# Moving the start address of one class of TensorE operands from 192 to 64 bytes (modulo 512) behind the next stationary tile

## The chip, the cores and the metric

The program runs on one core of a Trainium2 chip. The metric is device time in microseconds of one execution; the median of three runs of the kernel before is 938.64 us.

## What is computed

Four residual layers on a sequence of 256 tokens of width 1024, batch 1, all in float32. Layer 0 mixes with gated linear attention, layer 1 with differential attention; each is followed by a SwiGLU feed-forward block (width 2816) and a gated per-layer-embedding block. Then come a short gated convolution and a causal attention with linear biases and an output gate. Cut to what matters here:

```python
def swiglu(h, w_in, w_out):
    g, u = split_cols(h @ w_in, [D_FF, D_FF])
    return (jax.nn.silu(g) * u) @ w_out

q, k, v, r, zf, zb = split_cols(h @ w_in, ...)      # gated linear attention
q, k, v = split_cols(h @ w_in, ...)                 # differential attention
h = h + mixer(rms_norm(h, g), ...)
```

Almost all arithmetic is in the products of a 256 x 1024 (or 256 x 2816) activation with a weight matrix. The kernel keeps float32 accuracy by splitting both sides in a high part (rounded to the matmul format fp32r) and a low part (the rest), and adding three products: high x high, high x low, low x high.

## The kernel before

Weights come from HBM in pieces ("units") of at most 128 x 1024 values on SP's queue into the tile `raw` (`load`, L151). ScalarE rounds a piece into the high part `whi` (`high`, L165, instruction at L169), VectorE subtracts it from the piece for the low part `wlo` (`low`, L173, instruction at L178). Both run some units ahead of TensorE. A table of due times (`DL`) sets where the elementwise steps of a mixer stand between the units. None of this order depends on an address.

`gemm` (L227) turns a weight matrix into units. A unit of four 256-column pieces gives 24 matmuls: four pieces, two halves `s`, and three products in `mm3` (L222 to L225). There are two forms. In the usual form the weights are stationary (128 x 128 tiles of `whi` and `wlo`) and the activations move (`xh`, `xl`, 256 columns). In the `natural` form, used where the result must have tokens on partitions, it is the other way round: a 128 x 128 tile of `xh` or `xl` is stationary and 256 columns of `whi` or `wlo` move. The natural form is used for four chunks of `gla_i` (the values of the first mixer), all twelve of `diff_i` and twelve of `moba_i`: 28 chunks of two units, each with 24 matmuls, so 448 times the triple

- L223: stationary `xh`, moving `whi`
- L224: stationary `xh`, moving `wlo`
- L225: stationary `xl`, moving `whi`

TensorE loads the stationary tile of a matmul (LDWEIGHTS, PEld in the profile) while the matmul before it still streams its moving operand. In the program's names, `g<-whi,xh` has the moving operand first.

`shifted` (L159) places the weight tiles. Each gets 1152 values (4608 bytes, nine times 512) and begins at an offset `o` in its slot, so that all buffers of a pool have the same start modulo 512. With `DIST = 192` and `SLOT = 512` the moving weights begin 192 bytes into the slot; stationary weights begin at 512 - 192 = 320 bytes, so that the activations that move over them, at 0, are again 192 bytes behind them modulo 512. The activation tiles `xh` and `xl`, and all slices of 128 columns in them, begin at multiples of 512 bytes; a piece of 256 columns is 1024 bytes. So every matmul of both forms moves an operand that begins 192 bytes (modulo 512) behind the stationary tile that is loaded meanwhile. The score products of the attention stages use the same `mm3` with `kh`, `kl` moving over `qh`, `ql`; those tiles all begin at multiples of 512 bytes, a distance of 0.

Of the kernel before, what the change touches and what calls it, by code (L numbers as in the profile page):

```python
# [86 lines left out]
DIST = 192  # L87
SLOT = 512
# [7 lines left out]
def body(ctx: ExitStack, tc: tile.TileContext, a, out: bass.AP):  # L96
# [62 lines left out]
    def shifted(pool, name, u):  # L159
        key, j = seq[u][:2]  # L160
        moving = key == "diff_i" or key == "gla_i" and 4 <= j < 8 or key == "moba_i" and j < 12
        o = (DIST if moving else SLOT - DIST) // 4
        return pool.tile([P, CW // 2 + SLOT // 4], F32R, tag=name, name=name)[:, o:o + CW // 2]

    def high():  # L165
        u = state["hi"]
        key, j, k0, kn, c = seq[u]
        hi = shifted(whip, "whi", u)
        nc.scalar.copy(hi[:, :kn * c], raws[u][:, :kn * c])  # L169
        his[u] = hi  # L170
        state["hi"] += 1

    def low():  # L173
        u = state["lo"]
        key, j, k0, kn, c = seq[u]
        hi = his.pop(u)
        lo = shifted(wlop, "wlo", u)
        nc.vector.tensor_sub(lo[:, :kn * c], raws.pop(u)[:, :kn * c], hi[:, :kn * c].bitcast(F32))  # L178
        ready[u] = [(hi[:, k * c:(k + 1) * c], lo[:, k * c:(k + 1) * c]) for k in range(kn)]
        state["lo"] += 1  # L180
# [1247 lines left out]
```

## Time and profile before

| | us |
|---|---|
| median of 3 runs (lowest, highest) | 938.64 (937.60, 939.99) |
| the profiled execution's own time | 937.24 |
| its span | 935.1 |
| TensorE busy in the span | 913.7 |
| VectorE busy | 663.4 |
| ScalarE busy | 556.2 |
| GpSimd busy | 107.3 |
| mean granted TensorE clock | 0.992 |

The profile is one execution of the program. The duration of a matmul in it includes its latency and overlaps that of the next; how long one really takes of TensorE's time is the distance between two starts, which the timeline shows. That distance is called a step below. The chain of waits names, from the end backwards, what each instruction waited for last.

### The profile page before, as it was taken

How to read it: one execution, taken by the hardware profiler on the slowest of the kernel's cores; microseconds unless marked ns; L12 is line 12 of the kernel's file. 1: busy time of each engine (PE TensorE's matmuls, PEld its weight loads, DVE VectorE, ACT ScalarE, POOL GpSimd, SP SyncE). 2: the span in 40 equal slices, each digit the busy share in tenths (PEclk: the TensorE clock that was granted, in tenths of full speed). 3: DMA queues.
4: the chain of work that ended last, by engine and by line, in shares of the span. 5: the costliest groups of instructions: out<-in, count | busy, mean ns of one | idle time of the engine just before them, and what ended most of it. 6: DMA issues, size and time to landing. Idle time of an engine off the chain costs nothing.

```text
span 935.1 us, 19090 instructions
## 1 busy us (share of the span) xinstructions
PE 913.7 (98%) x7812; PEld 900.6 (96%) x7812; DVE 663.4 (71%) x1000; ACT 556.2 (59%) x951; POOL 107.3 (11%) x74
## 2 busy tenths in 40 slices
PE   9889999999999989899999999999999999999998
PEld 8889999999999989899999999999999999999998
DVE  5884768666656698998587666566897668876663
ACT  5945757455444565677585545444774445777862
POOL 0050310000001352211010000012210003000010
PEclk9989999999999998999999999999999999999999
DMA  8543366655555734343466555565556546644332
GB/s 243 200 138 107 109 205 230 211 189 195 181 189 190 241 127 149 122 141 108 146 217 215 199 193 193 177 200 195 168 206 201 192 132 205 186 134 136 113 114 90
DMA packets 48151, 161.10 MB, mean 172 GB/s; under 512 B 5472, under 2 KB 6368, under 8 KB 48064
## 3 DMA queue, kind: packets, MB, share of 16 engines
q1 hardware_dynamic: 47376, 158.81, 51.7%
q8 instruction: 61, 1.00, 0.4%
q10 hardware_dynamic: 688, 1.07, 0.4%
q14 instruction: 26, 0.21, 0.1%
HBM read 158.81 MB, written 1.05 MB: 171 GB/s over the span
## 4 chain that ended last, share of the span: by engine, by line
PE 81%; DVE 10%; ACT 4%; POOL 2%; issue 2%; DMA 2%; SPq 0%; ACTq 0%; POOLq 0%; DVEq 0%
PE g L223 25%; PE g L225 24%; PE g L224 24%; DVE wlo L178 3%; ACT whi L169 1%; PE m L223 1%; PE m L818 1%; DVE xl L305 1%; PE m L996 1%; DMA h<-in_xT 1%; PE m L1196 1%; PE m L653 1%; ACT xh L301 1%; PE m L224 1%; DVE q L600 1%
## 5 line engine op out<-in xcount | busy, mean ns | idle before, releaser
L223 PE MATMUL g<-xh,whi 128*128 128x256 f32 (+1 forms) x1672 | 465.7, 279 | 1.3 <-ACT whi L169 0.7
L225 PE MATMUL g<-xh,wlo 128*128 128x256 f32 (+1 forms) x1672 | 462.5, 277 | 0.2
L224 PE MATMUL g<-xl,whi 128*128 128x256 f32 (+1 forms) x1672 | 462.4, 277 | 0.1
L178 DVE TENSOR_TENSOR wlo<-raw,whi 128x1024 fp32r<-128x1024 f32 (+2 forms) x315 | 377.3, 1203 | 80.3 <-PE g L225 43.8
L169 ACT CAST whi<-raw 128x1024 fp32r<-128x1024 f32 (+2 forms) x315 | 312.0, 996 | 117.6 <-PE g L224 93.4
L223 PEld LDWEIGHTS g<-xh,whi 128*128 128x128 f32 (+1 forms) x1672 | 314.1, 188 | 2.4 <-ACT whi L169 1.0
L225 PEld LDWEIGHTS g<-xh,wlo 128*128 128x128 f32 (+1 forms) x1672 | 313.8, 188 | 0.6 <-DVE wlo L178 0.6
L224 PEld LDWEIGHTS g<-xl,whi 128*128 128x128 f32 (+1 forms) x1672 | 313.7, 188 | 0.6 <-DVE xl L305 0.3
L223 PE MATMUL g<-whi,xh 128*128 128x256 f32 x448 | 130.8, 292 | 3.5 <-ACT xh L301 3.5
L225 PE MATMUL g<-whi,xl 128*128 128x256 f32 x448 | 127.1, 284 | 0.2 <-DVE xl L305 0.2
L224 PE MATMUL g<-wlo,xh 128*128 128x256 f32 x448 | 126.9, 283 | 0.0
L223 PEld LDWEIGHTS g<-whi,xh 128*128 128x128 f32 x448 | 86.8, 194 | 5.2 <-ACT xh L301 4.0
L225 PEld LDWEIGHTS g<-whi,xl 128*128 128x128 f32 x448 | 86.6, 193 | 0.6 <-DVE xl L305 0.6
L224 PEld LDWEIGHTS g<-wlo,xh 128*128 128x128 f32 x448 | 86.5, 193 | 0.0
L494 ACT ACTIVATE t<-t 128x256 f32<-128x256 f32 x44 | 18.5, 420 | 85.7 <-DVE t L482 85.6
L223 PE MATMUL g<-ah,whi 128*128 128x256 f32 x224 | 61.8, 276 | 0.0
L224 PE MATMUL g<-al,whi 128*128 128x256 f32 x224 | 61.8, 276 | 0.0
L225 PE MATMUL g<-ah,wlo 128*128 128x256 f32 x224 | 61.8, 276 | 0.0
L482 DVE TENSOR_TENSOR t<-g,rb 128x256 f32<-128x256 f32 x44 | 18.6, 424 | 52.1 <-PE g L225 52.0
L305 DVE SCALAR_TENSOR_TENSOR xl<-h,small,xh 128x256 fp32r<-128x256 f32 x64 | 36.6, 610 | 17.1 <-ACT xh L301 17.1
L301 ACT ACTIVATE xh<-h,small 128x256 fp32r<-128x256 f32 x64 | 29.3, 503 | 32.1 <-DVE h L466 7.9
L379 POOL TENSOR_TENSOR h<-h,pj 128x512 f32<-128x512 f32 x8 | 12.9, 1621 | 276.6 <-DVE h L395 270.8
(224 smaller groups left out, 1010.0 us busy)
## 6 DMA issues: line engine op xcount, KB each, us to landing
raw<-in_ffn_i SPq DMA_DIRECT2D x88, 512.0 KB, 4.6
raw<-in_ffn_o SPq DMA_DIRECT2D x40, 512.0 KB, 4.0
raw<-in_conv_i SPq DMA_DIRECT2D x32, 512.0 KB, 4.6
raw<-in_moba_i SPq DMA_DIRECT2D x32, 512.0 KB, 3.8
raw<-in_diff_i SPq DMA_DIRECT2D x24, 512.0 KB, 3.8
raw<-in_gla_i SPq DMA_DIRECT2D x23, 512.0 KB, 5.1
raw<-in_ple_g SPq DMA_DIRECT2D x16, 512.0 KB, 4.7
raw<-in_gla_o SPq DMA_DIRECT2D x5, 512.0 KB, 4.0
```

The costliest lines, as they stand in the source:

```text
L169: nc.scalar.copy(hi[:, :kn * c], raws[u][:, :kn * c])
L178: nc.vector.tensor_sub(lo[:, :kn * c], raws.pop(u)[:, :kn * c], hi[:, :kn * c].bitcast(F32))
L223: nc.tensor.matmul(ps, lh, rh, start=first, stop=False, **kw)
L224: nc.tensor.matmul(ps, lh, rl, start=False, stop=False, **kw)
L225: nc.tensor.matmul(ps, ll, rh, start=False, stop=last, **kw)
L301: nc.scalar.activation(xh[:, j], h[:, j], AF.Copy, scale=gain[j])
L305: nc.vector.scalar_tensor_tensor(xl[:, j], h[:, j], gain[j], xh[:, j].bitcast(F32), op0=ALU.mult, op1=ALU.subtract)
L379: nc.gpsimd.tensor_add(n, h, proj[p // 3][i])
L482: nc.vector.tensor_mul(g, ps[:, 0], N.rb)
L494: chain(layer, ("fs", lambda: nc.scalar.activation(sg, g, AF.Silu)), ("fm", lambda: nc.vector.tensor_mul(t3, sg, ps[:, 1])), ("fh", lambda ...
L600: nc.vector.tensor_mul(Q[:, :, 0::2], q16.rearrange("p (m n) c -> p m n c", n=2), ep.rearrange("p (m n) c -> p m n c", n=2))
L653: nc.tensor.matmul(ps[:, d, :192], S.kk[d].rearrange("p (m n) c -> p m (n c)", n=2)[:, 2 * h + t], S.q3[d][:, 2 * h + t].rearrange("p n c ...
```

## The change

The high part of moving weights begins 64 bytes into its slot, the low part still 192. Stationary weights stay where they were.

```diff
     def shifted(pool, name, u):
         key, j = seq[u][:2]
         moving = key == "diff_i" or key == "gla_i" and 4 <= j < 8 or key == "moba_i" and j < 12
-        o = (DIST if moving else SLOT - DIST) // 4
+        o = (DIST if moving and name == "wlo" else 64 if moving else SLOT - DIST) // 4
         return pool.tile([P, CW // 2 + SLOT // 4], F32R, tag=name, name=name)[:, o:o + CW // 2]
```

The pools have the same sizes and buffers, and the instructions of every engine stand in the same order as before.

## Rows read from the trace of the kernel before

**Rows 1.** The page, busy time of the engines.
```profile
PE 913.7 (98%) x7812; PEld 900.6 (96%) x7812; DVE 663.4 (71%) x1000; ACT 556.2 (59%) x951; POOL 107.3 (11%) x74
```
**Rows 2.** Groups by line: line, engine, out<-in, count | busy us, mean ns | idle before.
```profile
L223 PE MATMUL g<-xh,whi 128*128 128x256 f32 x1664 | 463.3, 278 | 0.6 <-ACT xh L301 0.6
...
L223 PE MATMUL g<-whi,xh 128*128 128x256 f32 x448 | 130.8, 292 | 3.5 <-ACT xh L301 3.5
L225 PE MATMUL g<-whi,xl 128*128 128x256 f32 x448 | 127.1, 284 | 0.2 <-DVE xl L305 0.2
L224 PE MATMUL g<-wlo,xh 128*128 128x256 f32 x448 | 126.9, 283 | 0.0
```
**Rows 3.** Timeline of PE (start us, duration us, what), feed-forward block of layer 0.
```profile
145.80 0.28 PE L225 MATMUL g<-xh,wlo 128*128 128x256 f32 x1
...
324.64 0.28 PE L225 MATMUL g<-xh,wlo 128*128 128x256 f32 x1
```
**Rows 4.** Timeline of PE, start and end of the moving weights of `gla_i`.
```profile
39.52 0.28 PE L225 MATMUL g<-xh,wlo 128*128 128x256 f32 x1
39.63 0.28 PE L223 MATMUL g<-whi,xh 128*128 128x256 f32 x1
39.75 0.28 PE L224 MATMUL g<-wlo,xh 128*128 128x256 f32 x1
...
53.89 0.29 PE L224 MATMUL g<-wlo,xh 128*128 128x256 f32 x1
```
**Rows 5.** Timeline of PE, moving weights of `diff_i`.
```profile
371.55 0.28 PE L225 MATMUL g<-whi,xl 128*128 128x256 f32 x1
...
373.59 0.28 PE L225 MATMUL g<-whi,xl 128*128 128x256 f32 x1
```
**Rows 6.** Groups of the chain of waits, four stretches in order of time: 39.5:61.6, 376:390, 402:440, 796.5:877.4.
```profile
by line: DVE q L600 22.4%; issue 20.5%; DVE wlo L178 10.5%; POOL q L604 8.6%; DVE b L572 7.8%; DVE la L565 5.6%; DVE kk L609 5.5%; ACT ab L561 5.3%; ACT ab L560 4.3%; PE m L653 3.1%; DVE qk L641 2.6%; ACT ab L555 1.7%; ACT la L556 1.6%; DVE
...
by line: DVE wlo L178 21.7%; DVE e L968 17.5%; DVE w L961 10.1%; DVE m L893 9.5%; DVE mx L941 8.7%; issue 8.6%; DVE ss L799 4.3%; DVE m L888 4.3%; DVE ql L829 4.3%; DVE kl L829 4.3%; DVE w L960 2.5%; DVE nb L943 2.3%; DVE ms L801 1.2%; DVE 
...
by line: PE g L223 23.4%; PE g L224 21.7%; PE g L225 21.7%; PE m L996 10.9%; PE m L223 5.7%; PE m L818 4.6%; PE m L224 4.3%; PE m L975 4.1%; PE m L225 3.7%
...
by line: PE g L223 25.1%; PE g L224 23.9%; PE g L225 23.9%; PE m L223 6.0%; PE m L818 5.5%; PE m L1196 4.7%; PE m L224 3.4%; PE m L225 3.4%; PE m L1212 2.6%; PE m L1214 1.1%; PE m L343 0.3%; issue 0.0%
```
**Rows 7.** PE's waits over the whole span, two of the longest.
```profile
PE m L653 <- POOL q L604: 2.1, 1, 2.1
PE m L818 <- POOL ro L901: 1.9, 1, 1.9
```
**Rows 8.** Busy time by stretch, of instructions that use `whi`, on PE.
```profile
402.00:440.00 38.00, 27.03 (x144) 1.00 0.42 138
796.50:877.40 80.90, 62.61 (x336) 1.00 0.46 145
```
**Rows 9.** Timeline of PE, score products of the differential attention.
```profile
374.60 0.28 PE L223 MATMUL m<-kh,qh 64*128 64x256 f32 x1
...
374.84 0.28 PE L225 MATMUL m<-kh,ql 64*128 64x256 f32 x1
```
**Rows 10.** Timeline of PE, products in plain float32 (seven records merged).
```profile
437.50 0.94 PE L996 MATMUL m<-v,aT 128*128 128x128 f32 x7
```
**Rows 11.** Timeline of PE, a stretch in which the granted clock was 0.5.
```profile
62.31 0.41 PE L225 MATMUL g<-whi,xl 128*128 128x256 f32 x1
...
66.58 0.41 PE L224 MATMUL g<-wlo,xh 128*128 128x256 f32 x1
```
**Rows 12.** Timeline of PE, early steps of a unit with stationary weights (`moba_i`).
```profile
898.36 0.29 PE L224 MATMUL g<-xl,whi 128*128 128x256 f32 x1
898.49 0.29 PE L225 MATMUL g<-xh,wlo 128*128 128x256 f32 x1
```
**Rows 13.** Busy time by stretch of VectorE's subtraction at L178.
```profile
150.00:320.00 170.00, 77.00 (x64) 1.00 0.60 199
...
363.50:437.40 73.90, 23.97 (x19) 1.00 0.40 129
```

## The prediction

> **What bounds the kernel now.** I read the page first: TensorE is busy for 913.7 us, 98% of the span, against 71% on VectorE [rows 1]. So time is to be had or lost mostly in the steps of its matmuls. The groups by line then show which matmuls the change touches: the three groups with moving weights, 448 each; two of them (L223 and L225) move `whi`, 896 matmuls in all, and L224 moves `wlo` [rows 2]. Their durations in the profile contain latency, so the cost of one is taken from the distance of two starts in the timeline.
>
> Those starts show that a step has two lengths, in both forms of product, with the same addresses. In the feed-forward block 1,578 steps in a row take 178.84 us, 113.3 ns each [rows 3]. In `gla_i` 121 steps with moving weights take 14.26 us, 117.8 ns each [rows 4]; in `diff_i` 18 steps take 2.04 us, 113.3 ns each again [rows 5]. Once a run of steps has either length it keeps it, mostly until other work on TensorE breaks it. All these steps have a distance of 192 bytes. So the distance alone doesn't fix the step: something that is carried from step to step does too.
>
> Last I read the chain of waits by stretch, since a longer step costs nothing where TensorE isn't what ends the stage. In `gla_i` the chain runs over VectorE, ScalarE and GpSimd, without a matmul with moving weights among its large shares (first row of [rows 6]), and TensorE then waits 2.1 us for GpSimd's `q` [rows 7]. In the first half of the differential attention it runs over VectorE (second row of [rows 6]), and TensorE waits 1.9 us for `ro` [rows 7]. From 402 to 440 us and through the three projections of the last attention, 796.5 to 877.4 us, it runs over L223 to L225 (third and fourth row of [rows 6]). There a step counts in full. `whi` moves in 144 matmuls of the first of these stretches and in 336 of the second [rows 8]: 480. Of these, 437 are followed within 130 ns by another matmul with moving weights; the other 43 stand at a break, where the work that comes next sets the gap. Counted from the starts in the timeline, 296 of the 437 steps last 113 to 115 ns, 133 last 116 to 120 and 8 more than that; the mean is 114.9 ns. In the same stretches 240 such steps move `wlo`, with a mean of 115.0 ns.
>
> **The change, part by part.** No instruction, wait, byte or buffer is added, taken away or moved in order, so no queue is passed. Three things could change.
>
> First, the steps that move `whi`: 437 on the path, now 114.9 ns. The trace of before has no step at a distance of 64 bytes, so the price is bounded by the nearest rows.
> - From above: the score products move `kh` and `kl` at a distance of 0 and take two steps in 0.24 us [rows 9], 118 and 120 ns, 119 on average. The longest step without a wait in a run of products is 127 ns [rows 12].
> - From below: plain float32 products at a distance of 0 take (0.94 - 0.28) / 6 = 0.11 us, 111 ns [rows 10]. At half the clock (granted 0.5, the 1.2 GHz level) 20 steps with moving weights take 4.27 us, 213 ns each [rows 11]; half of that, 107 ns, is what 256 columns would take at 2.4 GHz if nothing else cost anything. No step can be shorter.
>
> I take 119 ns. It is the one row at another distance with the same format and the same 256 columns, and the plain float32 rows differ in format and width. There is a second sign: where stationary weights give way to moving ones, one step moves `xh` while a tile of `xh` is loaded, a distance of 0; it lasts 113 ns itself, but the run behind it falls to 117.8 [rows 4], from 113.3 in the run ahead of it, and the two other such places in the trace, where the second and third of these stages begin, do the same. A step at another distance thus seems to throw a run out of the short length. With two of three steps at 64 bytes, that would happen all the time. The sum: 437 x (119 - 114.9) = 1.8 us. At the ends: 437 x (127 - 114.9) = 5.3 us more, or 437 x (114.9 - 107) = 3.5 us less.
>
> Second, the steps that move `wlo` keep their distance. If they follow the others into the long length, 240 x (117.8 - 115.0) = 0.7 us more; into the short one, 240 x (115.0 - 113.3) = 0.4 us less. I take 0 and keep both for the range.
>
> Third, ScalarE writes and VectorE reads `whi` at another address. VectorE's subtraction takes 77.00 / 64 = 1.20 us where both parts begin at 320 and 23.97 / 19 = 1.26 us where they begin at 192 [rows 13]; other work differs too between these stretches. Where VectorE is the chain, at most 8 + 19 of them lie on it: 27 x 0.06 = 1.6 us either way. I take 0, because no row ties the difference to the address.
>
> The steps that I cost at nothing (`gla_i`, and `diff_i` up to 402 us) are hidden by VectorE's chain and the waits behind it. If that cover were gone, 130 steps moving `whi` in `diff_i` and 95 in `gla_i` (counted as above), each 4 ns longer, would add 0.9 us.
>
> The profiled execution took 937.24 us, 2.1 us of it outside its span; the median of the runs shown is 938.64, 1.4 us more. I add the sum to the median: 938.6 + 1.8 = **940.4 us**. About 0.3% (2.8 us) is what a measurement of this kernel can tell from no change, so this forecast reads as no change, with a lean to slower.
>
> **The rivals.**
>
> *Nothing happens (938.6 us).* For it speaks that 192 bytes gives both lengths [rows 3 to 5] and that plain float32 is at its 111 ns although its operands coincide modulo 512 [rows 10]; against it, the 119 ns at a distance of 0 in the same format. The Trainium skill has a rule for this case (TensorE: Matmul & The Clock Gate, section "Step-by-step: what each phase is for"): TensorE reads moving data and weights over two independent ports, and loading the next weights doesn't steal bandwidth from the running matmul. By that rule no distance matters and the sum is 0. The two lengths of a step at full clock agree with it badly, as something adds 6 to 11 ns to 107.
>
> *Faster.* 64 bytes keeps the runs in the short length or goes below it. At 113.3 ns on all steps it gives 437 x 1.6 + 240 x 1.7 = 1.1 us, 937.5; at 111 ns for `whi` 1.7 + 0.4 = 2.1 us, 936.5; at 107 ns 3.5 + 0.4 = 3.9 us, 934.7. Only near the last does it pass 0.3%. For it: 141 of the 437 steps are longer than they would have to be. Against it: the three groups of 1,664 with stationary weights (the first of them in [rows 2]) never go below 113 ns in a run.
>
> *Slower by more than can be overlooked.* The two reads meet in every load so late that the whole delay falls on the next matmul, as in the 127 ns step [rows 12]. It decides from 114.9 + 2800 / 437 = 121.3 ns a step. At 127 ns it is 5.3 us, with the `wlo` steps long as well 6.0 us, 944.6; with the cover on VectorE's stages gone, 225 x 12 = 2.7 us more, 947.3. For it: short steps above 120 ns occur now and then. Against it: they stay single, no run of them exists.
>
> *The change doesn't do what it says.* All `whi` buffers are 4608 bytes long, a multiple of 512, and the activation tiles too, so every `whi` slice lies at 64 and every `wlo` slice at 192. I give this no chance.
>
> **How the numbers follow.** Forecast (`whi` steps at about 119 ns) 0.40; nothing happens 0.22; faster 0.18; clearly slower 0.20. Faster by over 0.3% is half of the faster case and a little measurement spread, 0.10. Slower by over 0.3% is most of the slower case, 0.17, and the part of the forecast in which the `wlo` steps follow or the cover is gone, 0.08: together 0.25. The rest, 0.65, is within 0.3%. The range leaves out the ends of the last two cases: from 935.8, between the 111 and the 107 ns cases, to 944.2, at 127 ns with `wlo` unchanged.
>
> **What the profile after would show.** Right: 448 matmuls each at L223 to L225 as before; in the timeline, steps from a `whi` matmul of 117 to 120 ns nearly everywhere in 402 to 440 and in the last attention, and runs at 113 ns gone; the feed-forward blocks unchanged at 113.3 ns; the waits on GpSimd in the first and third stage a little shorter. Wrong: steps of `whi` still in two kinds of run at 113 and 118 (nothing happens), any run below 113 (faster), or above 121 (slower).

## The result: slower by 0.92%, most of it in a block that the change does not touch

The changed kernel takes 946.97 us (median; 944.79 to 948.58) against 938.12 us before: ratio 1.0092, 95% interval 1.0064 to 1.0120. The forecast was 940.4 us.

The profile after, its span and the busy time of the engines (the second line answers to [rows 1]):

```profile
span 946.4 us, 19090 instructions
...
PE 927.3 (98%) x7812; PEld 913.6 (97%) x7812; DVE 664.0 (70%) x1000; ACT 556.0 (59%) x951; POOL 108.6 (11%) x74
```

Same instructions, same work on the other engines; TensorE is busy 13.6 us longer. The groups by line of the changed kernel (line, engine, out<-in, count | busy us, mean ns) show where, and it isn't where the change was made:

```profile
L223 PE MATMUL g<-xh,whi 128*128 128x256 f32 x1664 | 467.8, 281 | 0.6 <-ACT xh L301 0.6
...
L223 PE MATMUL g<-whi,xh 128*128 128x256 f32 x448 | 130.5, 291 | 3.2 <-ACT xh L301 3.2
L225 PE MATMUL g<-whi,xl 128*128 128x256 f32 x448 | 127.5, 285 | 0.2
L224 PE MATMUL g<-wlo,xh 128*128 128x256 f32 x448 | 126.1, 281 | 0.0
```

Beside [rows 2], the three groups with moving weights hardly differ, although two thirds of their steps got longer, as shown below: the busy time of a group is made of durations that overlap, and isn't the sum of its steps. The stationary group went from 463.3 to 467.8 us, though no address in it was changed.

Busy time of PE in three stretches, each inside one block with stationary weights: feed-forward of layer 0, feed-forward of layer 1, convolution (us, busy, count of matmuls that lie in or reach into the stretch, clock, DMA). Before:

```profile
150.00:310.00 160.00, 160.00 (x1414) 1.00 0.60 199
490.00:650.00 160.00, 160.00 (x1414) 1.00 0.60 197
705.00:775.00 70.00, 70.00 (x620) 1.00 0.53 173
```

After:

```profile
150.00:310.00 160.00, 160.00 (x1415) 1.00 0.60 200
490.00:650.00 160.00, 160.00 (x1361) 1.00 0.58 188
705.00:775.00 70.00, 70.00 (x597) 1.00 0.54 178
```

The count is the reading: 160 us plus the 0.28 us of the one that reaches in, over 1,414, is a step of 113.4 ns (the starts give 113.3); over 1,361 it is 117.8. So the block of layer 0 stays in the short length, and that of layer 1 and the convolution are in the long one. The timeline of PE after says it without rounding by counts; this run answers to [rows 3], in the other feed-forward block:

```profile
481.10 0.28 PE L224 MATMUL g<-xl,whi 128*128 128x256 f32 x1
...
667.42 0.28 PE L225 MATMUL g<-xh,wlo 128*128 128x256 f32 x1
```

1,582 steps in 186.32 us: 117.8 ns. The starts of the two profiled executions, laid beside each other matmul by matmul, divide the 11.3 us between their spans as follows: 2.3 us gained up to 367 us, in the first mixer and at the start of the differential attention, where VectorE's chain sets the time; 0.6 us lost again up to 388 us and 0.6 from there to 460; 7.8 us lost from 460 us to the end of the feed-forward block of layer 1 (1,578 steps and a run of 177 ahead of it, 4.4 ns each); 3.9 us lost in the convolution; 0.8 us in the last attention. The convolution's share is chance, as the runs below show: it comes out either way at the same addresses. The 7.8 us are not.

The steps that the change does touch, after, in the last attention (timeline of PE; answers to [rows 5]):

```profile
807.88 0.28 PE L224 MATMUL g<-wlo,xh 128*128 128x256 f32 x1
...
815.41 0.28 PE L225 MATMUL g<-whi,xl 128*128 128x256 f32 x1
```

64 steps in 7.53 us, 117.7 ns each, and so nearly everywhere: over the two stretches on the path (now 401 to 439 and 806.8 to 888 us) 436 steps that move `whi`, picked as in the prediction, have a mean of 118.4 ns, 8 of them still short, and 238 that move `wlo` have 116.5.

### The profile page after: what moved, and what is told of

The parts are those of the page before. It is cut to its first block, busy times and chain, and to the rows that moved or that the text cites. A ratio compares the mean times of both kernels' runs of the same rounds, so it can differ in the third digit from the quotient of the medians.

```text
span 946.4 us, 19090 instructions
## 1 busy us (share of the span) xinstructions
PE 927.3 (98%) x7812; PEld 913.6 (97%) x7812; DVE 664.0 (70%) x1000; ACT 556.0 (59%) x951; POOL 108.6 (11%) x74
## 4 chain that ended last, share of the span: by engine, by line
PE 80%; DVE 10%; ACT 3%; DMA 3%; POOL 2%; issue 2%; SPq 0%; ACTq 0%; POOLq 0%; DVEq 0%
PE g L223 24%; PE g L225 24%; PE g L224 24%; DVE wlo L178 3%; DMA raw<-in_gla_i 2%; PE m L223 1%; ACT whi L169 1%; PE m L818 1%; PE m L996 1%; DVE xl L305 1%; DMA h<-in_xT 1%; PE m L1196 1%; ACT xh L301 1%; PE m L224 1%; PE m L653 1%
## 5 line engine op out<-in xcount | busy, mean ns | idle before, releaser
L224 PE MATMUL g<-xl,whi 128*128 128x256 f32 (+1 forms) x1672 | 467.2, 279 | 0.3 <-DVE xl L305 0.2
L225 PE MATMUL g<-xh,wlo 128*128 128x256 f32 (+1 forms) x1672 | 467.2, 279 | 0.1
L178 DVE TENSOR_TENSOR wlo<-raw,whi 128x1024 fp32r<-128x1024 f32 (+2 forms) x315 | 375.9, 1199 | 85.3 <-PE g L225 48.7
L225 PEld LDWEIGHTS g<-xh,wlo 128*128 128x128 f32 (+1 forms) x1672 | 317.7, 190 | 0.8 <-DVE wlo L178 0.8
```

Source lines behind the costliest of these rows:

```text
L224: nc.tensor.matmul(ps, lh, rl, start=False, stop=False, **kw)
L225: nc.tensor.matmul(ps, ll, rh, start=False, stop=last, **kw)
```

## The experiments

Two theories were put against each other and against the plain price of the change. A: a long step that arises at 64 bytes is handed on to the runs behind. B: in a stretch in which TensorE waits for nobody, the lengths of all its steps are fixed by the sequence of instructions and addresses, so any change in the stretch deals a new, fixed hand: another set of lengths, the same in every execution. C: 64 bytes costs something by itself and nothing else happens.

### One stage at a time

In `shifted`, for one key of the three:

```diff
-        o = (DIST if moving else SLOT - DIST) // 4
+        o = (64 if moving and name == "whi" and key == "moba_i" else DIST if moving else SLOT - DIST) // 4
```

> Only the high parts of moba_i begin at 64 bytes; gla_i and diff_i are as before. Theory A (a long step that arises with moving weights is handed on to the long runs of stationary weights behind it): all long stationary runs but the short end lie ahead of this stage, so only its own steps lengthen, from about 115 to 118 ns on 306 steps: +1 us. Theory B (which length a long run falls into is drawn afresh at each break, by the exact timing there): the same +1 us, feed-forward and convolution blocks at 113 ns, since nothing ahead of the stage changes. Theory C (64 bytes is dear by itself): a third to a half of the whole change, +3 to +5 us.

> Only the high parts of diff_i begin at 64 bytes. Theory A: the runs behind it (feed-forward block of layer 1, convolution) go to 118 ns, so nearly the whole change: +7 to +9 us. Theory B: a new draw for these runs, anything from 0 to +11 us, with runs of 113 and of 118 in one execution. Theory C: +2 to +4 us, with the stationary runs at 113 ns.

> Only the high parts of gla_i begin at 64 bytes. These steps are hidden behind VectorE's chain. Theory A: the feed-forward block of layer 0 was at 113 ns with the whole change too, so nothing: 0 to -1 us. Theory B: a new draw for all long runs, 0 to +15 us, with some run at 118 ns. Theory C: 0.

`moba_i` alone: 937.76 us, ratio 1.0006 (0.9981 to 1.0030). `gla_i` alone: 937.67 us, 1.0005 (0.9982 to 1.0029). `diff_i` alone: 948.00 us, 1.0105 (1.0056 to 1.0155, four executions), the whole loss. Counts of PE with `diff_i` alone, in the feed-forward block of layer 1 and the convolution:

```profile
490.00:650.00 160.00, 160.00 (x1360) 1.00 0.57 188
705.00:775.00 70.00, 70.00 (x620) 1.00 0.53 180
```

The block is long, the convolution short in this execution. With `moba_i` or `gla_i` alone it is the other way round in their profiles (1,414 and 596), although neither touches anything between the two. The convolution's run begins behind waits of TensorE, and which length it gets varies. The block of layer 1 does not vary with it. For `gla_i` alone theory B had expected some long run at 118 ns by a new draw; both feed-forward blocks stay short.

The starts tell why. Neither kernel has any wait of TensorE from 402 us to the end of that block. Over this stretch the profiled executions of the kernel before, of `moba_i` alone and of `gla_i` alone agree step by step: a few steps up to 406 us differ by up to 11 ns, and from there on more than 2,200 agree within 1 ns. Those of the changed kernel and of `diff_i` alone agree with each other in the same way, on another sequence. TensorE does the same thing there in each of these executions.

The two sequences also show that the length is not simply handed on. Between `diff_i` and the block stand the first runs of `diff_o`, the output projection of this attention, whose addresses the change doesn't touch. The first of them, 22 steps, takes 2.59 us before and 2.49 us after:

```profile
441.19 0.28 PE L224 MATMUL g<-px,whi 128*128 128x256 f32 x1
...
443.78 0.29 PE L225 MATMUL g<-px,wlo 128*128 128x256 f32 x1
```

```profile
440.12 0.28 PE L224 MATMUL g<-px,whi 128*128 128x256 f32 x1
...
442.61 0.28 PE L225 MATMUL g<-px,wlo 128*128 128x256 f32 x1
```

So behind the long steps of the changed `diff_i` this run is short, where it was long before; the next one does the same (114.0 ns a step over the whole run against 117.6), and the long length comes back after them. The run behind the long block, from 668.1 us, is short again.

### An extra product on TensorE

Ahead of the first feed-forward block, addresses as before:

```diff
+                if (p, i - len(units)) in [(0, -2)]:
+                    bump = pm()
+                    for _ in range(1):
+                        nc.tensor.matmul(bump[:, 0, :P], ones, ones, start=True, stop=True)
                 turn(fn)
```

> All addresses as before (192 everywhere); one more 128-column float32 product of ones is issued on TensorE ahead of the last unit but one of the first mixer, two records of 0.11 us. Theory A: no distance changes, so the runs stay at 113 ns: +0.2 us. Theory B: the start of every long run behind it moves, so some of them fall into 118 ns: up to +15 us (feed-forward 7 us each, convolution 4 us). Theory C: +0.2 us.

937.42 us, ratio 0.9999 (0.9971 to 1.0026), both feed-forward blocks short. This change of timing doesn't make the run behind it long. It is one draw, for the block of layer 0 alone (TensorE waits between it and 402 us), and so a weak sign against B in its strong form, in which every change deals an even chance.

The same product inside the stretch from 402 to 661 us, with the addresses of before (128 and 32 columns) and with those of the change (128 and 64 columns). It also takes one of the five buffers behind `pm()`, so that later tiles `m` come one buffer further on; weights, activations and the sums `g` keep theirs.

```diff
+                if p == 2 and i == len(units) - 5:
+                    nc.tensor.matmul(pm()[:, 0, :128], ones, ones[:, :128], start=True, stop=True)
                 turn(fn)
```

> Addresses as before; one float32 product of ones (128 columns, 0.2 us) is issued on TensorE ahead of the fifth unit from the end of diff_o, so inside the stretch from 402 to 661 us in which TensorE waits for nobody. Theory A (64 bytes makes long steps and these are handed on): the feed-forward block of layer 1 stays at 113 ns, +0.2 us. Theory B (in a stretch without a wait the lengths of all steps are fixed by the sequence of instructions and addresses, so any change in it deals a new, fixed hand): the block may fall into 118 ns, then +7 us in all executions; over the four runs of this call with a bump, some flip.

> The same place, with 32 columns in place of 128. Theory A: 113 ns, +0.1 us. Theory B: another hand, 0 or +7 us, independent of the one of the 128-column product.

> The whole change, with the 128-column product at the same place. Theory A: the run ahead of it is long and hands its length on, so the feed-forward block stays at 118 ns and the time at about 947 us. Theory B: the block may come back to 113 ns, then about 940 us.

> The whole change, with 64 columns at the same place. Theory A: 118 ns, about 947 us. Theory B: about 947 or about 940 us, by the draw.

With the addresses of before nothing moves: 938.26 us, 1.0001 (0.9967 to 1.0034), and 938.20 us, 1.0006 (0.9977 to 1.0035). With those of the change the 7 us are won back: 939.85 us, 1.0009 (0.9973 to 1.0045), and 939.84 us, 1.0018 (0.9992 to 1.0044). The timeline of PE of the whole change with 128 columns, at the extra product (L1297), and the count in the block behind it:

```profile
461.26 0.28 PE L225 MATMUL g<-xh,wlo 128*128 128x256 f32 x1
461.38 0.39 PE L1297 MATMUL m<-ones 128*128 128x128 f32 x2
461.52 0.36 PE L223 MATMUL g<-xh,whi 128*128 128x256 f32 x1
```

```profile
490.00:650.00 160.00, 160.00 (x1415) 1.00 0.58 195
```

Up to the product the run steps at 118 ns; five steps behind it there are 150 at 113, and the block follows at 113. So A falls in its simple form as well: long steps of `diff_i` don't force the block into the long length, since 0.2 us of other work ahead of it is enough to end it. Not every piece of other work does that. In the changed kernel without the extra product, the two products at L338 stand between the run of 177 and the block, and both are long:

```profile
480.55 0.60 PE L338 MATMUL m<-ssum,ones 128*128 128x256 f32 x2
```

What is left is B with an uneven draw: the hand is fixed, the short length is the usual one for these long runs, and the change dealt a bad one.

The pair also gives an estimate of the price of the change without the block: 939.85 less 938.22, 1.6 us, with intervals that reach no change.

### Which units of `diff_i`

```diff
+        late = j in (7, 9, 10, 11) or j == 3 and k0 > 0
-        o = (DIST if moving else SLOT - DIST) // 4
+        o = (64 if key == "diff_i" and name == "whi" and late else DIST if moving else SLOT - DIST) // 4
```

and the same with `not late`.

> High parts at 64 bytes in the last nine units of diff_i alone, those that TensorE works on after its last wait (at about 401 us) ahead of the feed-forward block of layer 1. Theory B (the lengths of the steps in a stretch without a wait are fixed by what stands in it): the steps from there on are those of the whole change, the block at 118 ns in every execution: about 8 us more than before. If the 15 units ahead of the wait matter, the block stays at 113 ns: about +1 us.

> High parts at 64 bytes in the first 15 units of diff_i alone, those ahead of the wait. Theory B: the stretch behind the wait holds the instructions and addresses of before, so the block stays at 113 ns, and the units ahead of the wait are hidden behind VectorE: within 1 us of before. If long steps ahead of the wait are handed on over it, +7 us.

The nine late units alone: 946.99 us, 1.0107 (1.0076 to 1.0137, two executions). The fifteen early ones alone: 938.34 us, 1.0003 (0.9967 to 1.0040). Counts of PE in the block of layer 1, late units, then early units:

```profile
490.00:650.00 160.00, 160.00 (x1361) 1.00 0.56 187
```

```profile
490.00:650.00 160.00, 160.00 (x1414) 1.00 0.59 195
```

The steps with the late units agree with those of the changed kernel within 1 ns from 405 us to the end of the block, and the steps with the early units with those of the kernel before from 406 us on, more than 2,200 each. What stands ahead of TensorE's last wait, at about 401 us, plays no part. That is what B expects, and a handing on of long steps over the wait is ruled out.

### The distance by itself

Stationary weights at 64 bytes' distance, moving ones as before:

```diff
-        o = (DIST if moving else SLOT - DIST) // 4
+        o = (DIST if moving else SLOT - 64) // 4
```

> The price of 64 bytes by itself, on many steps: stationary weights begin at 448 bytes in place of 320, so the activations that move over them are 64 bytes behind; moving weights at 192 as before. If a distance of 64 has no short length (as the moving steps after the change suggest, 118 ns throughout), the three groups of 1,664 steps and the smaller ones, some 5,700, go from mostly 113.3 to 117.8 ns: +22 to +25 us, 960 us, and both feed-forward blocks stand at 118. If 64 bytes has both lengths like 192 and the moving steps are long for another reason (the alternation of 64 and 192), about 938 to 950 us with runs at 113 ns.

951.92 us, ratio 1.0187 (1.0157 to 1.0217, two executions). Counts of PE in the three blocks:

```profile
150.00:310.00 160.00, 160.00 (x1361) 1.00 0.56 188
490.00:650.00 160.00, 160.00 (x1361) 1.00 0.56 190
705.00:775.00 70.00, 70.00 (x620) 1.00 0.57 195
```

Both expectations miss in part. 64 bytes has the short length too: 887 steps of the convolution's run are at 113 ns. But it is the rare one: both feed-forward blocks and all other runs of over 22 steps with stationary weights are at 118. At 192 bytes the block of layer 0 was short in each of the other profiles.

High and low parts of moving weights both at 64, with the product in `diff_o`:

```diff
-        o = (DIST if moving else SLOT - DIST) // 4
+        o = (64 if moving else SLOT - DIST) // 4
```

> High and low parts of moving weights both at 64 bytes, with the 128-column product in diff_o that brought the feed-forward block of layer 1 back to 113 ns. If the distance is what makes the moving steps long, they stay at 118 ns and the time is that of the change with this product, about 940 us. If the alternation is, the moving steps have both lengths again and the time is about 938 us.

937.24 us against 934.99 for the kernel before on that chip, ratio 1.0032 (1.0015 to 1.0049). On the path the steps are long but for two units, with a mean of 117.6 ns for `whi` and 117.4 for `wlo`, counted from the starts in the stretches 397 to 438 and 796 to 878 us. In the hidden `gla_i` they are all short, 144 in a row, seen in the count of PE from 40 to 55 us:

```profile
40.00:55.00 15.00, 15.00 (x134) 1.00 0.41 136
```

So on the path it is the 64 bytes that favour the long length, with or without an alternation to 192; `gla_i`, mostly long at 192 and at the alternation, shows that this is no rule for every run.

### A version that might beat both

Addresses of before, and the 128-column product twice early in the convolution's run and once early in the program's last run:

```diff
+                if (p, i - len(units)) in [(4, -38), (4, -34), (5, -10)]:
+                    nc.tensor.matmul(pm()[:, 0, :128], ones, ones[:, :128], start=True, stop=True)
                 turn(fn)
```

> Addresses as before, with the extra 128-column product at three places: twice early in the run of the convolution, which is at 113 ns in some executions and at 118 in others (886 steps, 3.9 us), and once early in the last run of the program, at 118 ns in every profile so far (190 steps, 0.8 us). If a break of this kind brings a run back to the short length, as it did in four of four runs in diff_o, the time is 0.6 us of extra work more and 0.8 + about half of 3.9 us less: -2 us, 936 us, with a smaller spread. If it only draws anew, 938 to 939 us with the spread of before.

933.47 us against 934.99, ratio 0.9987 (0.9971 to 1.0002). The "four of four" of the expectation is too much: with the addresses of before, the run was short ahead of the product already, so only two of the four show a return. The last run of the program is short now; counts of PE in it before, and with the products:

```profile
912.00:925.00 13.00, 13.00 (x113) 1.00 0.32 102
```

```profile
912.00:925.00 13.00, 13.00 (x117) 1.00 0.29 102
```

The gain is in the expected direction, but its interval reaches no change: by the two ratios to the kernel before it beats the changed kernel, and it isn't shown to beat the one before.

## Why the prediction was wrong

- *What bounds the kernel* held: TensorE's steps, in two lengths at one and the same distance [rows 3 to 5]. The clause that something is carried from step to step was right, and the sum made no use of it.
- *The steps that move `whi`*: 437 x (119 - 114.9) = 1.8 us was forecast; 118.4 ns was measured, 437 x (118.4 - 114.9) = 1.5 us. The nearest row that was taken, the score products at a distance of 0 [rows 9], was close, in part by luck: nothing tied a distance of 0 to one of 64. The second sign for it doesn't hold as a rule: with both parts at 64, the same step at a distance of 0 stands ahead of the 144 steps of `gla_i`, and they stay short. Of the 437, 11 are followed by another kind of product and not by one with moving weights; without them the means are 114.8 and 118.4.
- *The steps that move `wlo`* were taken at 0 with 0.7 us as an end; they went from 115.0 to 116.5 ns, 238 x 1.5 = 0.4 us. Together 1.9 us; the runs with the extra product fit it with 1.6 us, but aren't clear of no change.
- *ScalarE and VectorE* at another address: taken at 0, and VectorE's busy time is 664.0 us against 663.4, which shows no effect.
- *The hidden stages* held: `gla_i` alone and the first 15 units of `diff_i` alone change nothing that can be measured.
- **The step that failed** is the list of what could change: it had the steps with moving weights, the low parts among them, and the two other engines, and said of the rest that the feed-forward blocks would stay at 113.3 ns. The block of layer 1 and the run ahead of it went to 117.8: 7.8 us, four times the whole forecast sum. The two-length rule had been read from the trace, also that a step of another distance throws a run out of the short length [rows 4], and it was applied only to the runs that have the new distance. That TensorE doesn't wait between these runs and the end of the block could have been read from its waits, and with it the risk that the block's length hangs on what stands ahead of it; which way it would go could not.
- The rival "clearly slower" had the right sign for a wrong reason: it asked for steps of 121 ns and more in the moving products, and there are none in a run. The sum of its range is off as well: 938.6 + 5.3 is 943.9 and not 944.2, which changes nothing here.
- The rule of the Trainium skill on two independent ports (TensorE: Matmul & The Clock Gate, "Step-by-step: what each phase is for") has no place for any of this. By it no distance matters. The run with stationary weights at 64 bytes, in which only the start of the stationary tiles differs, is 1.87% slower: here the measurement decides.

What stays open: what it is that TensorE carries from step to step, and why the extra product of 0.2 us ends it. Only distances of 0, 64 and 192 bytes were seen, and in each run one operand moved while the other stayed, so it isn't shown that the distance counts and not the start itself, nor that it counts modulo 512. The agreement within 1 ns rests on one profiled execution of each kernel. Single executions of the kernel before took 944 to 945 us, 1 of 25, 1 of 27 and 1 of 9 in three of the comparisons, and 1 of 8 with the 128-column product at the addresses of before; that the block of layer 1 was long in these fits the 7 us, but they have no trace. If it was, the same instructions and addresses don't always give the same lengths.

## What to carry to other kernels

Read the cost of a matmul from the distance of two starts, and count in long windows: two lengths 4% apart can hide under one mean. Where TensorE ran for 250 us without a wait, its steps came out the same to the nanosecond, but for a few at the head, in every profiled execution with the same instructions and addresses there, and a small edit at the head of the stretch set the speed of a block behind it; before a loss or gain is put down to the edit itself, look at the blocks that it doesn't touch, and try it with a harmless extra instruction behind it.

## What was not expected of the hardware

- Back-to-back fp32r products of 128 x 128 by 256 columns, each with a load of a new stationary tile, run at 113.3 or at 117.8 ns a step at the same addresses, and hold the one or the other for up to 1,582 steps.
- The start of an operand shifts which of the two is usual: with the moving operand 192 bytes (modulo 512) behind the stationary tile that is loaded meanwhile, both feed-forward blocks were at 113 ns in the profile before; at 64 bytes both were at 118, for 1.9% of the time.
- One float32 product of 0.2 us, put into a run at 118 ns, left it at 113 behind it; in the last run of the program and in `diff_o` alike, in each of the four profiles that have one there (with 64 columns in one of them, 128 in the others).
